# Moving columns of the last rows from VectorE to GpSimd, and recutting the last row

## The chip, the cores and the metric

One core of a Trainium2 chip. The metric is the device time of one execution in microseconds. One execution of each kernel is also profiled; it gives the trace, whose span is 1.77 us shorter than the time of the same execution (628.57 against 626.8 for the kernel before). A load's *landing* is the moment of its last completion event in the trace.

## The reference

```python
def setup_inputs():
    return {"x": np.random.randn(8192, 8192).astype(np.float32)}

def reference(x):
    return np.linalg.norm(x, ord=np.inf, axis=1)
```

That is the largest absolute value of each row of 268 MB of float32. Every byte is read once and 32 KB are written.

## The kernel before

The kernel handles 128 rows of x at a time, one per partition (a "row" below is such a group of 8192 columns per partition; a "pair" is two of them in one transfer). SyncE issues all loads into a ring of three pairs, and VectorE takes the absolute maximum along the columns. For the last pair and the last two rows GpSimd helps: ScalarE makes the values positive in place, then GpSimd takes the maximum of their bits as integers. The constants give, per transfer, its columns and GpSimd's share of them:

```python
TILES = (
    [[(8192, 0)]] * HEAD
    + [[(16384, 0)]] * (PAIRS - 1)
    + [[(16384, 7168)], [(8192, 3328)]]
    + [[(4160, 1760), (2080, 832), (1024, 384), (512, 0), (416, 0)]]
)
```

VectorE gets the rest of each transfer. The last row comes in five pieces. Each share of it leaves one partial maximum behind the last piece's columns in the tile `last`, and one final reduce takes the piece and the partial maxima together:

```python
            if final:                                   # the last piece of the last row
                pairs_out()
                absmax(res[:, R - 1 :], last)           # its columns and the partial maxima
            elif u == len(TILES) - 1:                   # the other pieces of the last row
                for eng, a, e in ((absmax, 0, w - g), (absmax_pool, w - g, w)):
                    if a < e:
                        i = w_last + n_part
                        red = eng(last[:, i : i + 1], buf[:, a:e])
                        n_part += 1
                        # (cut: the matmuls of warm())
            # (cut: whole rows for VectorE alone)
            else:                                       # the last pair, and the row before the last
                part = single.tile([P, 2], FP32, name=f"part{u}")
                c = w // n_cols - 1
                if c:
                    absmax(res[:, row : row + c], buf[:, : c * n_cols])
                red = absmax(part[:, 0:1], buf[:, c * n_cols : w - g])
                absmax_pool(part[:, 1:2], buf[:, w - g :])
                max_pool(res[:, row + c : row + c + 1], part)
```

After the final reduce TensorE transposes the last four rows' results, ScalarE copies them out of PSUM and a small store ends the kernel.

## Time and profile before

| kernel before | |
|---|---|
| time, median of 3 (lowest, highest) | 628.57 us (628.52, 628.62) |
| span of the profiled execution | 626.8 us |
| start of VectorE's 8192 reduce of the last pair | 603.28 us |
| end of the final reduce | 624.14 us |
| between the two, called the **tail** below | 20.86 us |
| end of the final reduce to end of span | 2.66 us |

The first 603 us are a stream of loads, which the change doesn't touch. What the change can move is the tail. It is worked out from lines rounded to 0.01 us. The time of an execution is the sum 603.28 + 20.86 + 2.66 + 1.77 = 628.57. The profile's lines are read in the prediction.

### The profile page before, as it was taken

Reading aid. Unit: us, or ns where it says so; the run is one execution under the profiler, and the core shown is the slowest. Engines: PE = TensorE matmul, PEld = TensorE weight load, DVE = VectorE, ACT = ScalarE, POOL = GpSimd, SP = SyncE. Lnnn points to the kernel's source line nnn. Section 1 sums busy time; section 2 is a strip of 40 time slices with the busy share of each in tenths; the row PEclk is TensorE's granted clock in tenths of the full one; section 3 lists DMA queues with packets and bytes.
Section 4 is the critical chain, followed back from the end, with each engine's and each line's share of the span. In section 5 each row is a group of like instructions: output and inputs, shape, how many; then the busy total and the mean of one; then the engine's idle time right before and its main releaser. Section 6 shows DMA issues by size and latency. Waiting matters only on the chain.

```text
span 626.8 us, 218 instructions
## 1 busy us (share of the span) xinstructions
PE 8.7 (1%) x15; PEld 3.2 (1%) x15; DVE 537.5 (86%) x39; ACT 14.3 (2%) x10; POOL 13.3 (2%) x13
## 2 busy tenths in 40 slices
PE   0000000000000000000000000000000000000005
PEld 0000000000000000000000000000000000000002
DVE  1938988889988889888898888988889988889888
ACT  0000000000000000000000000000000000000034
POOL 0000000000000000000000000000000000000007
PEclk9999999999999999999999999999999999999999
DMA  8999999999999999999999999999999999999996
GB/s 368 435 468 402 468 402 468 402 468 402 468 402 468 402 460 410 452 418 448 422 448 422 418 452 402 468 402 468 402 468 402 468 402 468 402 468 402 460 402 278
DMA packets 5525, 268.47 MB, mean 428 GB/s; under 512 B 627, under 2 KB 789, under 8 KB 1045
## 3 DMA queue, kind: packets, MB, share of 16 engines
q1 hardware_dynamic: 5472, 268.44, 99.1%
q10 hardware_dynamic: 53, 0.03, 0.0%
HBM read 268.44 MB, written 0.03 MB: 428 GB/s over the span
## 4 chain that ended last, share of the span: by engine, by line
DMA 70%; DVE 29%; issue 0%; SPq 0%; PE 0%; ACT 0%; DVEq 0%
DMA ring<-in_x_dram 70%; DVE res L64 28%; DVE part L64 1%; DVE last L64 1%; SPq L153 0%; PE ps_ones L189 0%; ACT sb_ones L190 0%; DVEq L64 0%
## 5 line engine op out<-in xcount | busy, mean ns | idle before, releaser
L64 DVE TENSOR_REDUCE res<-ring 128x2 f32<-128x16384 f32 (+1 forms) x32 | 525.4, 16420 | 86.5 <-DMA ring<-in_x_dram 86.5
L82 ACT ACTIVATE ring<-ring 128x7168 f32<-128x7168 f32 (+4 forms) x5 | 12.2, 2449 | 577.0 <-DMA ring<-in_x_dram 577.0
L71 POOL TENSOR_REDUCE part<-ring 128x1 int32<-128x7168 int32 (+1 forms) x2 | 9.1, 4566 | 587.3 <-ACT ring L82 587.2
L108 PE MATMUL ps_warm<-ident 128*128 128x512 f32 (+1 forms) x12 | 8.2, 827 | 614.5 <-DVE part L64 613.2
L64 DVE TENSOR_REDUCE part<-ring 128x1 f32<-128x1024 f32 (+1 forms) x2 | 6.3, 3210 | 0.0
L108 PEld LDWEIGHTS ps_warm<-ident 128*128 128x128 f32 x12 | 2.9, 274 | 618.8 <-issue 615.3
L64 DVE TENSOR_REDUCE last<-ring 128x1 f32<-128x2400 f32 (+3 forms) x4 | 5.3, 1392 | 0.0
L71 POOL TENSOR_REDUCE last<-ring 128x1 int32<-128x1760 int32 (+2 forms) x3 | 3.0, 1017 | 0.4 <-ACT ring L82 0.4
L96 ACT ACT_TABLE_LOAD x1 | 1.3, 1283 | 31.5 <-DVE res L64 31.5
L64 DVE TENSOR_REDUCE res<-last 128x1 f32<-128x423 f32 x1 | 0.6, 594 | 0.1
L88 POOL MEMSET ident<- 128x128 f32 x1 | 0.2, 205 | 21.4 <-DVE res L64 21.4
L128 ACT COPY sb_pairs<-ps_pairs 30x128 f32<-30x128 f32 x2 | 0.4, 254 | 0.0
L71 POOL TENSOR_REDUCE res<-part 128x1 int32<-128x2 int32 x2 | 0.4, 196 | 0.1
L123 PE MATMUL ps_pairs<-ident,res 128*30 128x128 f32 x2 | 0.4, 272 | 0.0
L190 ACT COPY sb_ones<-ps_ones 4x128 f32<-4x128 f32 x1 | 0.3, 255 | 2.0 <-PE ps_ones L189 2.0
masks.py:199 POOL TENSOR_SCALAR_AFFINE_SELECT ident<-ident 128x128 f32<-128x128 f32 x1 | 0.3, 294 | 0.1
L189 PE MATMUL ps_ones<-ident,res 128*4 128x128 f32 x1 | 0.3, 272 | 1.3 <-DVE res L64 1.3
L123 PEld LDWEIGHTS ps_pairs<-ident,res 128*30 128x30 f32 x2 | 0.2, 106 | 0.6 <-POOL res L71 0.3
L96 ACT ACTIVATE ident<-ident 128x1 f32<-128x1 f32 x1 | 0.2, 203 | 0.0
L208 POOL MEMSET const-float32-0.0<- 128x1 f32 x1 | 0.1, 99 | 0.2 <-issue 0.2
L208 POOL MEMSET const-bfloat16-1.0<- 128x1 bf16 x1 | 0.1, 102 | 0.0
L208 POOL MEMSET const-uint8-127<- 128x1 uint8 x1 | 0.1, 102 | 0.0
(2 smaller groups left out, 0.2 us busy)
## 6 DMA issues: line engine op xcount, KB each, us to landing
ring<-in_x_dram SPq DMA_DIRECT2D x3, 4096.0 KB, 21.5
ring<-in_x_dram SPq DMA_DIRECT2D x1, 2080.0 KB, 35.7
ring<-in_x_dram SPq DMA_DIRECT2D x1, 1040.0 KB, 37.8
ring<-in_x_dram SPq DMA_DIRECT2D x1, 512.0 KB, 38.5
ring<-in_x_dram SPq DMA_DIRECT2D x30, 40.8
ring<-in_x_dram SPq DMA_DIRECT2D x1, 256.0 KB, 38.7
last<-in_x_dram SPq DMA_DIRECT2D x1, 208.0 KB, 38.7
out_dram<-sb_pairs ACTq DMA_DIRECT2D x1, 30.0 KB, 1.5
```

Of the source, the lines that this page charges most:

```text
L64: return keep(nc.vector.tensor_reduce(out=dst, in_=src, axis=X, op=MAX, apply_absolute_value=True,)).ins
L71: keep(pool.add_instruction(mybir.InstTensorReduce(name=nc.get_next_instruction_name(), ins=[pool.lower_ap(src.bitcast(INT32))], outs=[poo ...
L82: keep(nc.scalar.activation(src, src, mybir.ActivationFunctionType.Abs))
L88: nc.gpsimd.memset(ident, 0.0).ins, after.name,
L96: abs_ident = nc.scalar.activation(ident[:, :1], ident[:, :1], mybir.ActivationFunctionType.Abs)
L108: product = keep(nc.tensor.matmul(ps_warm[:, : w * P], lhsT=ident, rhs=ident.unsqueeze(1).to_broadcast([P, w, P]), start=True, stop=True,) ...
L123: keep(nc.tensor.transpose(ps_pairs[r], both[:, :, r], ident))
L128: keep(nc.scalar.copy(sb[:, :, r], ps_pairs[r]))
L189: nc.tensor.transpose(ps_ones, res[:, X_ONE:], ident)
L190: keep(nc.scalar.copy(sb_ones, ps_ones))
L208: nc = _bacc.Bacc("TRN2", target_bir_lowering=False, num_devices=1)
```

## The change

Its intent is to relieve VectorE at the end of the kernel: GpSimd's shares grow by 2 to 8 per cent, and the last row is recut so that its last piece is larger and its first two smaller.

```diff
-    + [[(16384, 7168)], [(8192, 3328)]]
-    + [[(4160, 1760), (2080, 832), (1024, 384), (512, 0), (416, 0)]]
+    + [[(16384, 7328)], [(8192, 3488)]]
+    + [[(4128, 1824), (2048, 864), (1024, 416), (512, 0), (480, 0)]]
```

## The prediction

> **What bounds the kernel now.** I read four views in this order: the page's span and chain that ended last, the chain in order of time for the tail, the timeline of the last 24 us, and the groups by form for durations. The page says who holds the end in bulk:
>
> ```profile
> span 626.8 us, 218 instructions
> ...
> DMA 70%; DVE 29%; issue 0%; SPq 0%; PE 0%; ACT 0%; DVEq 0%
> ...
> q1 hardware_dynamic: 5472, 268.44, 99.1%
> ```
>
> The input queue keeps the 16 DMA engines busy 99.1% of the span. The 29% of VectorE (DVE) in the chain doesn't mean that VectorE bounds the stream: a load waits there for a ring buffer to be released, and other loads are in flight meanwhile. The change touches no load before the last row, so only the tail matters:
>
> ```profile
> 562.46 40.80 DMA ring<-in_x_dram
> ...
> 603.28 8.69 DVE res L64
> 611.97 6.25 DVE part L64 x2
> 618.22 5.25 DVE last L64 x4
> ...
> 623.55 0.60 DVE res L64
> ...
> 624.20 0.28 PE ps_ones L189
> ...
> 624.51 0.26 ACT sb_ones L190
> ```
>
> Columns: start, length, what. From 603.28 to 624.16 VectorE works with no gap. It is the engine that sets the end of the tail, and after it come only a transpose, a copy and the store. The timeline shows how close the others are:
>
> ```profile
> 603.28 8.69 DVE L64 TENSOR_REDUCE res<-ring 128x1 f32<-128x8192 f32 x1 [2.14 <-DMA ring<-in_x_dram]
> 603.36 6.18 ACT L82 ACTIVATE ring<-ring 128x7168 f32<-128x7168 f32 x1 [570.36 <-DMA ring<-in_x_dram]
> ...
> 613.04 2.98 ACT L82 ACTIVATE ring<-ring 128x3328 f32<-128x3328 f32 x1 [3.50 <-DMA ring<-in_x_dram]
> ...
> 617.97 1.67 ACT L82 ACTIVATE ring<-ring 128x1760 f32<-128x1760 f32 x1 [1.95 <-DMA ring<-in_x_dram]
> ...
> 619.71 3.08 POOL L71 TENSOR_REDUCE last<-ring 128x1 int32<-128x1760 int32 x3 [0.38 <-ACT ring L82]
> 620.45 0.90 ACT L82 ACTIVATE ring<-ring 128x832 f32<-128x832 f32 x1 [0.81 <-DMA ring<-in_x_dram]
> ...
> 621.68 0.52 ACT L82 ACTIVATE ring<-ring 128x384 f32<-128x384 f32 x1 [0.34 <-DMA ring<-in_x_dram]
> ```
>
> ScalarE (ACT) starts 0.02 to 0.07 us after a piece lands, so these lines give the landings. The landing events of the trace put them at 603.26 (last pair), 612.97 (8192 columns), 617.94 (4160), 620.43 (2080), 621.66 (1024), 622.29 (512) and 622.80 (416). GpSimd (POOL) ends its last reduce at 619.71 + 3.08 = 622.79. VectorE finishes its last partial reduce at 623.46 and starts the final one at 623.55. So before the final reduce the last landing has 0.75 us to spare and GpSimd 0.76 us: VectorE alone is late, and shifting columns to GpSimd is aimed at the right engine.
>
> The durations of one instruction (last number):
>
> ```profile
> L64 DVE TENSOR_REDUCE part<-ring 128x1 f32<-128x4864 f32 x1 | 5.2, 5209 | 0.0
> ...
> L64 DVE TENSOR_REDUCE last<-ring 128x1 f32<-128x512 f32 x1 | 0.7, 675 | 0.0
> ...
> L64 DVE TENSOR_REDUCE res<-last 128x1 f32<-128x423 f32 x1 | 0.6, 594 | 0.1
> ...
> L71 POOL TENSOR_REDUCE part<-ring 128x1 int32<-128x7168 int32 x1 | 6.2, 6164 | 587.2 <-ACT ring L82 587.2
> ...
> L71 POOL TENSOR_REDUCE last<-ring 128x1 int32<-128x384 int32 x1 | 0.5, 509 | 0.0
> ```
>
> VectorE: (5209 - 675) / (4864 - 512) = 1.042 ns a column plus 142 ns (the final one 153). GpSimd: (6164 - 509) / (7168 - 384) = 0.834 ns plus 189. ScalarE's 6176 ns for 7168 and 524 for 384 give 0.833 ns plus 204.
>
> **What the Trainium skill says.** "SBUF — State Buffer", section "Who interferes with whom": VectorE and GpSimd share a port pair, but a tensor_reduce on trn2 never takes it. The trace agrees: the 4864 reduce beside a busy GpSimd follows the same line (1.042 ns a column) as the 8192 reduce of an early row that ran without it (8686 ns, mean of three). So longer GpSimd shares should not slow VectorE. "Perfetto Trace Analysis", section "Optimizing Scalar/DVE Operations": about 60 ns of engine time for a VectorE instruction on SBUF, the profiled latency about twice that, the write-acknowledgement half overlapping the next. The trace agrees: the constant is 142 ns, and the next reduce starts 80 ns before the former ends (613.01 + 5.21 = 618.22 against a start at 618.14), which leaves 62. "TensorE: Matmul & The Clock Gate", Part 1: the array falls to half clock after an idle window of about 3.4 us. The warming matmuls end near 622.9 and the last transpose comes at 624.20, so the gap of 1.3 us is safe. "HBM Reference", Specifications: a core streaming alone measures about 425 GB/s; the page shows a mean of 428.
>
> **The change, part by part.** No instruction and no byte is added or removed. VectorE's own shares become 16384 - 8192 - 7328 = 864 (was 1024), 8192 - 3488 = 4704 (was 4864), 4128 - 1824 = 2304 (was 2400), 2048 - 864 = 1184 (was 1248), 1024 - 416 = 608 (was 640), 512 as before, and the final 480 + 7 partial maxima = 487 (was 423). That is 512 columns off VectorE and 64 back. At 1.042 ns, 448 columns would be 0.47 us if nothing else stood in the way. The landings do, once. I replay the tail, starting each reduce at the later of "0.08 before the former ends" and "0.02 after the landing" (603.28 against 603.26). Landings in the row of pieces move earlier by the columns no longer ahead of them, at (622.80 - 612.97) / 8192 = 1.20 ns a column: 0.04 us for the first piece, 0.08 for the next three, nothing for the last.
>
> - 864: starts 611.88 as before, lasts 0.90 + 0.14 = 1.04, ends 612.92; VectorE is free at 612.84, but the 8192 piece lands at 612.97. Of the 0.167 us won, only 0.02 is kept.
> - 4704: 612.99 + 5.04 = 618.03. Free at 617.95; landing 617.90. Won 0.167.
> - 2304: 617.95 + 2.54 = 620.49. Free at 620.41; landing 620.35. Won 0.100.
> - 1184: 620.41 + 1.375 = 621.785. Free at 621.705; landing 621.58. Won 0.067.
> - 608: 621.705 + 0.775 = 622.48. Free at 622.40; landing 622.21. Won 0.033.
> - 512: 622.40 + 0.675 = 623.075; the final starts 0.09 later, at 623.165; its piece is in at 622.80.
> - Final, 487: 0.507 + 0.153 = 0.66, ends 623.825. Lost 0.067.
>
> Sum: -0.02 - 0.167 - 0.100 - 0.067 - 0.033 + 0.067 = -0.32 us against the old end of 624.14. The transpose, copy and store follow unchanged. 628.57 - 0.32 = 628.25 us.
>
> GpSimd has to be checked on the same clock. ScalarE's 7328 ends at 603.36 + 6.31 = 609.67, GpSimd starts 0.07 later and takes 6.30, to 616.04; its small merge and the 3488 (3.10 us) follow by about 619.46; the second merge; the 1824 at about 619.78 (it now waits for GpSimd itself, no longer for ScalarE's 1824, done near 619.66). The three last shares are 128 columns longer, 0.107 us, so it ends near 619.78 + 3.08 + 0.11 = 622.97, 0.18 later than before and 0.2 before the final reduce can start. The slack is spent, not exceeded.
>
> **The rivals.** First, landings as the new bound. For it: after the change VectorE reaches the 4128 piece only 0.05 us after it lands, and the 8192 piece before it lands. Against it: a landing 0.1 us late would cost only the missing 0.05, because each later piece leaves more room. It would make about 628.3. Second, GpSimd as the last to finish. For it: its margin falls from 0.76 to about 0.2 us, and spans on it are rough. Against it: its durations lie on one line over 7168 to 384 columns. If it ran 0.4 us later than I have it, the final reduce would start 0.2 later: 628.45, still under the old time. Third, the larger final piece: the final reduce is the one step that can't lie beside anything, and 64 columns more cost 0.067 there; that is in the sum. Had VectorE been waiting for the last landing, this would be the whole effect, 628.64; the 0.75 us of slack speaks against it. Fourth, a change of the DMA stream by the new piece widths. Its 16-engine share is already 99.1%, and pieces of 4160, 2080 and 1024 columns landed at one pace (1.19 to 1.21 ns a column), so I expect nothing.
>
> **Range and chances.** The effect is 0.05%. The three runs before lie within 0.1 us, but 620 us of stream ahead of the tail may shift by some tenths in another run or on another chip, which is more than the effect. Hence 628.25, with 627.8 to 628.75 for 8 in 10. A 2% change is 12.6 us; nothing in the last 24 us can give it, and no earlier load is altered, so within 2% gets 0.99.
>
> **What would show it.** The profile after should have: an idle time of VectorE of about 0.1 us before the 4704 reduce, released by the DMA, and no other in the tail; the 487 reduce at about 660 ns; the gap from the start of the reduce at 603.28 to the end of the final one shorter by 0.3 us (20.86 to 20.54); GpSimd's last reduce ending 0.1 to 0.3 us before the final reduce starts. I am wrong if the final reduce waits for GpSimd or for a DMA, if the last transpose leaves its 272 ns, or if the landings from 603.26 to 622.80 (19.54 us) stretch by over 0.2 us.

## The result, and the profile after

| | before | after |
|---|---|---|
| time, median (lowest to highest), 6 runs each | 628.58 us (628.52 to 628.62) | 628.28 us (628.17 to 628.48) |
| start of the 8192 reduce | 603.28 | 603.39 |
| tail | 20.86 | 20.55 |
| end of final reduce to end of span | 2.66 | 2.66 |

The ratio is 0.9996 with a 95% interval of 0.9983 to 1.0009. (A ratio is the mean time of one kernel's runs over that of the other's of the same rounds, so not quite the ratio of the medians.) The medians differ by 0.30 us and the tails by 0.31. All six runs after lie below all six before (628.48 against 628.52), but the interval includes 1.

The chain of waits for the tail of the kernel after (start, length, what):

```profile
581.93 31.14 DMA ring<-in_x_dram
613.08 0.02 issue
613.10 5.05 DVE part L64
618.15 5.05 DVE last L64 x4
...
623.28 0.67 DVE res L64
```

Before, the chain ran on VectorE from 603.28 on. Now its VectorE part begins at 613.10, right after the landing of a load: the 8192 columns of the row before the last. VectorE was ready for them and waited. From there to 623.94 it has no gap but the 0.1 us before the final reduce, which was there before.

The timeline of the kernel after (start, length, engine, line, operation, shapes; in brackets idle time and what ended it):

```profile
603.39 8.69 DVE L64 TENSOR_REDUCE res<-ring 128x1 f32<-128x8192 f32 x1 [2.13 <-DMA ring<-in_x_dram]
...
618.00 1.72 ACT L82 ACTIVATE ring<-ring 128x1824 f32<-128x1824 f32 x1 [1.74 <-DMA ring<-in_x_dram]
...
619.79 3.04 POOL L71 TENSOR_REDUCE last<-ring 128x1 int32<-128x1824 int32 x3
```

GpSimd's last three shares end at 619.79 + 3.04 = 622.83, which is 0.45 us before the final reduce starts at 623.28. Its share of the 4128 piece starts 0.07 us after ScalarE has finished it (618.00 + 1.72 = 619.72).

The groups by form (the last two numbers before the second bar are busy us and mean ns, the last one idle us before it):

```profile
L71 POOL TENSOR_REDUCE part<-ring 128x1 int32<-128x7328 int32 x1 | 6.3, 6295 | 587.4 <-ACT ring L82 587.4
...
L64 DVE TENSOR_REDUCE part<-ring 128x1 f32<-128x4704 f32 x1 | 5.1, 5052 | 0.1
...
L64 DVE TENSOR_REDUCE last<-ring 128x1 f32<-128x2304 f32 x1 | 2.5, 2543 | 0.0
...
L64 DVE TENSOR_REDUCE res<-last 128x1 f32<-128x487 f32 x1 | 0.7, 660 | 0.1
```

The durations are within 0.01 us of the ones worked out beforehand: 5.05, 2.54 and 0.66 us for 4704, 2304 and 487 columns. The 0.1 us of idle time before the 4704 reduce is the wait for the landing.

### The profile page after: what moved, and what is told of

It is laid out like the page before. It is cut to its first block, busy times and chain, and to the rows that moved or that the text cites. A ratio compares the mean times of both kernels' runs of the same rounds, so it can differ in the third digit from the quotient of the medians.

```text
span 626.6 us, 218 instructions
## 1 busy us (share of the span) xinstructions
PE 8.5 (1%) x15; PEld 3.1 (0%) x15; DVE 537.1 (86%) x39; ACT 14.7 (2%) x10; POOL 13.5 (2%) x13
## 4 chain that ended last, share of the span: by engine, by line
DMA 70%; DVE 29%; SPq 0%; issue 0%; PE 0%; ACT 0%; DVEq 0%
DMA ring<-in_x_dram 70%; DVE res L64 28%; DVE part L64 1%; DVE last L64 1%; SPq L153 0%; PE ps_ones L189 0%; ACT sb_ones L190 0%; DVEq L64 0%
## 5 line engine op out<-in xcount | busy, mean ns | idle before, releaser
L82 ACT ACTIVATE ring<-ring 128x7328 f32<-128x7328 f32 (+4 forms) x5 | 12.6, 2524 | 576.5 <-DMA ring<-in_x_dram 576.5
L71 POOL TENSOR_REDUCE part<-ring 128x1 int32<-128x7328 int32 (+1 forms) x2 | 9.4, 4697 | 587.4 <-ACT ring L82 587.4
L64 DVE TENSOR_REDUCE part<-ring 128x1 f32<-128x864 f32 (+1 forms) x2 | 6.1, 3047 | 0.1
L64 DVE TENSOR_REDUCE last<-ring 128x1 f32<-128x2304 f32 (+3 forms) x4 | 5.1, 1342 | 0.0
L71 POOL TENSOR_REDUCE last<-ring 128x1 int32<-128x1824 int32 (+2 forms) x3 | 3.0, 1052 | 0.1
```

What stands on the lines that cost most here:

```text
L64: return keep(nc.vector.tensor_reduce(out=dst, in_=src, axis=X, op=MAX, apply_absolute_value=True,)).ins
L71: keep(pool.add_instruction(mybir.InstTensorReduce(name=nc.get_next_instruction_name(), ins=[pool.lower_ap(src.bitcast(INT32))], outs=[poo ...
L82: keep(nc.scalar.activation(src, src, mybir.ActivationFunctionType.Abs))
```

## The experiments

**Theory.** VectorE's chain of reduces sets the end. A column taken off it is worth 1.04 ns, unless VectorE then reaches a piece before it has landed; a column added to the final reduce costs as much. GpSimd has slack. **Rivals:** the new piece widths, not the shares, are what helped; every column off VectorE counts in full, landings or not; GpSimd is already at its limit, or its late start holds the end.

Each run below gives the tail of its profiled execution and the median of its timed ones. Unless it says otherwise, an edit is to the kernel after. The kernel before had a median of 628.66 us (628.54 to 629.19; nine runs in the first call, and these with one more in the second) and of 628.54 (628.38 to 629.17; the same nine runs serve the third and the fourth). Each tail is of one execution, and how far the tail of one kernel scatters was not measured. Four kernels from which the theory expects nearly the same tail (the kernel after, and the runs first_share_back, first_share_larger and shares_in_halves below) came out at 20.55 to 20.56 us.

### The two halves of the change by themselves

The shares without the new pieces:

```diff
-    + [[(4128, 1824), (2048, 864), (1024, 416), (512, 0), (480, 0)]]
+    + [[(4160, 1856), (2080, 896), (1024, 416), (512, 0), (416, 0)]]
```

> The larger GpSimd shares with the old pieces (4160, 2080, 1024, 512, 416): VectorE's partial reduces are those of the changed kernel (864, 4704, 2304, 1184, 608, 512) and its final one is 423 again. Tail = start of VectorE's 8192 reduce in the last pair to the end of the final reduce (20.86 us before, 20.55 after). My theory (VectorE's chain, cut short by landings): 0.07 us is saved on the final reduce, but the old pieces land 0.04 to 0.08 later, so VectorE waits some 0.03 us before the 2304 and again before the 1184 reduce; tail 20.53 to 20.57, 628.25 to 628.30 us, as good as the whole change. Rival 1 (the piece widths are what helped): tail near 20.86, 628.58. Rival 2 (VectorE's columns alone count, no landings): 20.55 - 0.07 = 20.48, 628.21.

Measured: tail 20.53 us; 628.27 us (628.22 to 628.30), ratio 0.9993 (0.9980 to 1.0007). The 2304 and 1184 reduces became 9 and 10 ns longer (2552 and 1386), which the theory does not name; they also start where VectorE meets the landing. From its timeline:

```profile
603.31 8.69 DVE L64 TENSOR_REDUCE res<-ring 128x1 f32<-128x8192 f32 x1 [2.12 <-DMA ring<-in_x_dram]
...
623.25 0.59 DVE L64 TENSOR_REDUCE res<-last 128x1 f32<-128x423 f32 x1
```

The pieces without the shares:

```diff
-    + [[(16384, 7328)], [(8192, 3488)]]
-    + [[(4128, 1824), (2048, 864), (1024, 416), (512, 0), (480, 0)]]
+    + [[(16384, 7168)], [(8192, 3328)]]
+    + [[(4128, 1760), (2048, 832), (1024, 384), (512, 0), (480, 0)]]
```

> The new piece widths with GpSimd's old shares: VectorE's partial reduces 1024, 4864, 2368, 1216, 640, 512 and a final 487, in sum as many columns as before (32 + 32 less, 64 more). My theory: tail 20.86 us, 628.58 us, no gain. Rival 1 (the piece widths are what helped, by the stream or by the landings): tail near 20.55, 628.28.

Measured: tail 20.86 us; 628.49 us (628.38 to 628.66), ratio 0.9997 (0.9985 to 1.0010). From its timeline:

```profile
603.10 8.69 DVE L64 TENSOR_REDUCE res<-ring 128x1 f32<-128x8192 f32 x1 [2.13 <-DMA ring<-in_x_dram]
...
623.30 0.66 DVE L64 TENSOR_REDUCE res<-last 128x1 f32<-128x487 f32 x1
```

In this profile, of an execution of 628.38 us, the 8192 reduce starts at 603.10, 0.18 us earlier than in the kernel before, so the 0.17 us between the medians lies in the stream ahead of the tail as far as the profiled execution can tell. What follows from the two: the shares give the whole gain. The new cut gives none. It does one thing that is hidden: the last landing comes 19.49 us after the pair's in this run and after, against 19.53 and 19.54 with the old widths, but nobody waits for it.

### Is each column off VectorE worth its time?

The last pair's share put back:

```diff
-    + [[(16384, 7328)], [(8192, 3488)]]
+    + [[(16384, 7168)], [(8192, 3488)]]
```

> The changed kernel with GpSimd's share of the last pair back at 7168, so that VectorE's 864 reduce is 1024 again. My theory: the wait of about 0.1 us for the 8192 piece before the 4704 reduce goes, and only 0.01 to 0.03 us is lost: tail 20.56 to 20.58 us, 628.28 to 628.31. Rival (every column taken off VectorE is worth its 1.04 ns): 160 columns, 0.17 us longer, tail 20.72, 628.45.

Measured: tail 20.56 us; 628.29 us (628.19 to 628.69), ratio 0.9995 (0.9983 to 1.0008). The groups by form of this run show no idle time before the 4704 reduce:

```profile
L64 DVE TENSOR_REDUCE part<-ring 128x1 f32<-128x4704 f32 x1 | 5.0, 5044 | 0.0
```

So 160 columns more on VectorE cost 0.01 us, not 0.17. And the other way, 320 columns fewer:

```diff
-    + [[(16384, 7328)], [(8192, 3488)]]
+    + [[(16384, 7648)], [(8192, 3488)]]
```

> The changed kernel with 320 more columns for GpSimd in the last pair (7648), so that VectorE's 864 reduce becomes 544. My theory: VectorE then waits some 0.45 us instead of 0.12 for the 8192 piece and the tail (start of VectorE's 8192 reduce in the last pair to the end of the final reduce) stays 20.55 us; GpSimd ends 0.26 us later and still ahead of the final reduce; 628.28 us. Rival (each column off VectorE is worth 1.04 ns): tail 20.22, 627.95. Rival (GpSimd is already at its limit): tail 20.8.

Measured: tail 20.55 us; 628.2 us (628.06 to 628.67), ratio 0.9993 (0.9981 to 1.0006). The timeline of VectorE in this run:

```profile
611.73 0.71 DVE L64 TENSOR_REDUCE part<-ring 128x1 f32<-128x544 f32 x1
612.84 5.05 DVE L64 TENSOR_REDUCE part<-ring 128x1 f32<-128x4704 f32 x1 [0.40 <-DMA ring<-in_x_dram]
```

The 0.33 us that the shorter reduce saves turn into idle time, and the profile names the load that ends it. A miss in the detail: GpSimd ended 19.86 us after the start of the 8192 reduce, 0.42 later than in the kernel after and not 0.26, so that it and VectorE were ready for the final reduce together. The expectation had counted the 320 columns on GpSimd alone; ScalarE's step on the share, which comes first, took 0.27 us longer too (6.58 us against 6.31), and a later wait for ScalarE that fell away took back some 0.13. Both runs tell the same: the gain of the kernel after is cut short at the landing of the 8192 piece, and what the last pair's share does beyond that is worth nothing.

### How near is GpSimd to its limit?

```diff
-    + [[(4128, 1824), (2048, 864), (1024, 416), (512, 0), (480, 0)]]
+    + [[(4128, 1984), (2048, 1024), (1024, 576), (512, 0), (480, 0)]]
```

> The changed kernel with 160 more columns for GpSimd in each of the 4128, 2048 and 1024 pieces (1984, 1024, 576). My theory: GpSimd takes the place of VectorE as the last before the final reduce. Its last reduce ends 0.40 us later (480 columns at 0.834 ns) and the final reduce waits for it, with VectorE also waiting 0.1 to 0.15 us at landings; tail 20.65 to 20.83 us, so slower than the changed kernel by 0.1 to 0.28: 628.38 to 628.56. Rival (VectorE's columns count alone): 480 columns, 0.50 us shorter, tail 20.05, 627.8. Rival (landings alone bound it): tail near 20.4, as VectorE then is ready 0.16 us earlier.

Measured: tail 20.69 us; 628.6 us (628.18 to 628.92), ratio 0.9998 (0.9986 to 1.0011). From the timeline of this run:

```profile
620.33 3.44 POOL L71 TENSOR_REDUCE last<-ring 128x1 int32<-128x1984 int32 x3 [0.22 <-ACT ring L82]
...
623.80 0.66 DVE L64 TENSOR_REDUCE res<-last 128x1 f32<-128x487 f32 x1 [0.41 <-POOL last L71]
```

VectorE's final reduce sits idle 0.41 us until GpSimd's last share is there (620.33 + 3.44 = 623.77). This is the first bracket of that kind on the final reduce. Beyond some size of the shares, then, more columns for GpSimd lengthen the tail, and 480 columns more are beyond it. A miss in the detail: GpSimd ended 0.55 us later than in the kernel after (20.00 us after the start of the 8192 reduce) and not 0.40; the bracket of 0.22 us shows that it waited for ScalarE, whose step on the larger share is longer as well.

```diff
-    + [[(16384, 7328)], [(8192, 3488)]]
-    + [[(4128, 1824), (2048, 864), (1024, 416), (512, 0), (480, 0)]]
+    + [[(16384, (3664, 3664))], [(8192, (1744, 1744))]]
+    + [[(4128, (896, 928)), (2048, (864,)), (1024, (416,)), (512, ()), (480, ())]]
```

(and a loop over the parts of a share, each with its own Abs, its own maximum and its own column among the partial maxima)

> The changed kernel with GpSimd's shares of the last pair, of the 8192 piece and of the 4128 piece each cut in two (3664 + 3664, 1744 + 1744, 896 + 928), so that GpSimd starts 3 us earlier, after ScalarE's first half. My theory (VectorE sets the end, GpSimd has slack): GpSimd gets idle time, ends about as before, VectorE's times don't change; tail 20.53 to 20.57, 628.28 us. Rival (GpSimd's late start is what holds the end): tail at least 0.1 us shorter, below 20.45.

Measured: tail 20.56 us; 628.23 us (628.17 to 628.44), ratio 0.9993 (0.9980 to 1.0007). GpSimd in this run:

```profile
606.59 6.43 POOL L71 TENSOR_REDUCE part<-ring 128x1 int32<-128x3664 int32 x2 [584.37 <-ACT ring L82]
...
614.66 3.23 POOL L71 TENSOR_REDUCE part<-ring 128x1 int32<-128x1744 int32 x2 [1.38 <-ACT ring L82]
...
618.81 1.84 POOL L71 TENSOR_REDUCE last<-ring 128x1 int32<-128x896 int32 x2 [0.53 <-ACT ring L82]
```

Counted from the start of the 8192 reduce (603.18 here, 603.39 there), it starts 3.05 us earlier than in the kernel after (3.41 us after it, not 6.46), and it gets idle time of 1.38 and 0.53 us instead, waiting for ScalarE, which waits for landings. The tail stays. GpSimd's late start doesn't hold the end.

### Versions meant to beat both

If VectorE reaches the final piece 0.4 us after it has landed, more columns may go from VectorE's earlier pieces to GpSimd and into the final piece. Constants only:

```diff
-    + [[(16384, 7328)], [(8192, 3488)]]
-    + [[(4128, 1824), (2048, 864), (1024, 416), (512, 0), (480, 0)]]
+    + [[(16384, 7328)], [(8192, 3552)]]
+    + [[(4064, 1824), (1984, 896), (1024, 480), (512, 0), (608, 0)]]
```

> Only the constants of the last rows: GpSimd 7328 and 3552; pieces 4064, 1984, 1024, 512, 608 with GpSimd 1824, 896, 480. My theory says that in the changed kernel the final piece lies in SBUF some 0.4 us before VectorE gets to it; so more columns can move from VectorE's earlier pieces to GpSimd and into the final piece until its reduce starts as it lands (VectorE 864, 4640, 2240, 1088, 544, 512, final 615). Expected: final reduce starts 0.3 us earlier than in the changed kernel and takes 0.79 us; tail 20.38 us (20.35 to 20.45), 628.08 to 628.15 us. Rival (the final piece must stay small, as its reduce lies beside nothing): tail 20.65 or more.

Measured: tail 20.39 us, the shortest of all; but 628.37 us (628.16 to 628.49), ratio 0.9995 (0.9981 to 1.0009). From its timeline:

```profile
603.56 8.69 DVE L64 TENSOR_REDUCE res<-ring 128x1 f32<-128x8192 f32 x1 [2.14 <-DMA ring<-in_x_dram]
...
623.16 0.79 DVE L64 TENSOR_REDUCE res<-last 128x1 f32<-128x615 f32 x1
```

The expectation for the tail holds and that for the time doesn't. In the profiled execution the stream was late: 603.56 + 20.39 + 2.65 + 1.77 = 628.37. The start of the 8192 reduce ranged from 603.10 to 603.77 over all profiled executions, more than any difference of tails here. So the median of five runs can't rank these versions.

Then the parts in halves, with a sixth piece to make the last reduces smaller:

```diff
-    + [[(16384, 7328)], [(8192, 3488)]]
-    + [[(4128, 1824), (2048, 864), (1024, 416), (512, 0), (480, 0)]]
+    + [[(16384, (5664, 1664))], [(8192, (1840, 1968))]]
+    + [[(4128, (832, 1088)), (1952, (512, 480)), (896, (544,)), (352, ()), (352, ()), (512, ())]]
```

> A version meant to beat both: GpSimd's large shares in two parts (5664 + 1664, 1840 + 1968, 832 + 1088, 512 + 480), and the last row in six pieces of 4128, 1952, 896, 352, 352 and 512 columns, so that VectorE reaches the final piece as it lands. VectorE 864, 4384, 2208, 960, 352, 352, 352 and a final 522. My theory: the final reduce starts within 0.05 us of the last landing and takes 0.70 us; tail 20.24 us (20.2 to 20.35), 627.95 to 628.05 us. Rivals: a sixth piece slows the last landings by over 0.1 us, or one of the shorter GpSimd parts comes late: tail 20.4 or more.

Measured: tail 20.44 us; 628.17 us (627.97 to 628.53), ratio 0.9993 (0.9979 to 1.0006). From its timeline:

```profile
623.16 0.70 DVE L64 TENSOR_REDUCE res<-last 128x1 f32<-128x522 f32 x1 [0.20 <-DMA last<-in_x_dram]
```

A miss: the final reduce waits for the last landing. That came at 623.03, 19.64 us after the pair's where the runs with five pieces had until then 19.47 to 19.54, and the reduce started 0.13 us after it, not 0.02. About 0.10 us of the 0.20 by which the tail missed its 20.24 are this wait (the idle time is 0.20 us, in the kernel after 0.10). The rest came earlier: the three reduces of 352 columns each started 0.02 to 0.03 us after their pieces had landed, and these landed late too. The first rival, a slower stream with a sixth piece, had come true in its number. Two runs went after its cause:

```diff
-    + [[(4128, 1824), (2048, 864), (1024, 416), (512, 0), (480, 0)]]
+    + [[(4128, 1824), (2048, 864), (1024, 416), (256, 0), (256, 0), (480, 0)]]
```

> The changed kernel with the 512 piece cut into 256 + 256, which adds one transfer and one VectorE reduce and leaves all else: a look at what a sixth piece costs by itself. In every run with five pieces the last landing came 19.47 to 19.54 us after the landing of the last pair; in the six-piece run 19.64. Theory A (a sixth transfer costs time in the stream): last landing 19.57 to 19.65 us after the pair's. Theory B (the widths of 352, 1952 and 896 columns in that run, or that run alone): 19.47 to 19.51. Either way VectorE sets the end, 0.06 us later than in the changed kernel for one more reduce: tail 20.60 to 20.63 us.

Measured (one look): tail 20.62 us, 628.29 us, last landing 19.51. A sixth transfer by itself cost the stream nothing to speak of here (19.51 against 19.49); the tail is longer by the one more reduce.

```diff
-    + [[(16384, 7328)], [(8192, 3488)]]
-    + [[(4128, 1824), (2048, 864), (1024, 416), (512, 0), (480, 0)]]
+    + [[(16384, (5664, 1664))], [(8192, (1808, 1808))]]
+    + [[(4096, (736, 1120)), (2048, (576, 448)), (896, (576,)), (384, ()), (384, ()), (384, ())]]
```

> The six-piece version again with widths in whole multiples of 128 columns (4096, 2048, 896, 384, 384, 384), a smaller final piece, and its shares set for a final reduce that starts 0.1 us after the last landing (GpSimd 5664 + 1664, 1808 + 1808, 736 + 1120, 576 + 448, 576). VectorE reaches the final reduce 19.71 us after the start of its 8192 reduce; it lasts 0.56. If the last landing is at 19.5 to 19.6 after the pair's: tail 20.27 to 20.32 us, about 628.0 to 628.1 us, the best of all. If the three small pieces land 0.1 us late or more, as in the first six-piece version, VectorE waits for each of them: tail 20.38 or more, no better than the version with retuned constants (20.39).

Measured: tail 20.49 us; 628.12 us (628.09 to 628.52), ratio 0.9993 (0.9979 to 1.0007). The last landing is at 19.74 us, later still, and VectorE started both of its 384 reduces 0.02 us after their pieces had landed, as the expectation had it for late landings. By its median this is the fastest kernel of the study, 0.42 us under the kernel before of the same call, but its interval too includes 1, and its tail is longer than that of the retuned constants. Even widths were no cure. The last two split the suspicion in two:

```diff
-    + [[(4128, 1824), (2048, 864), (1024, 416), (512, 0), (480, 0)]]
+    + [[(4096, 1792), (2048, 864), (1024, 416), (512, 0), (512, 0)]]
```

> A look at where the late last landing of the two six-piece versions comes from (19.64 and 19.74 us after the pair's, 19.47 to 19.54 in all the others). The changed kernel with pieces of 4096, 2048, 1024, 512 and 512 columns (GpSimd 1792, 864, 416): the 2048 piece now starts at column 4096, as in the even six-piece version, where it landed 2.53 us after the piece before it and not 2.43. If that start is the cause: 2.5 us again and a last landing at 19.55 or later. If not: 2.43 and 19.47 to 19.52. VectorE sets the end either way: tail 20.57 to 20.60 us.

Measured: tail 20.60 us, 628.4 us.

```diff
-    + [[(4128, 1824), (2048, 864), (1024, 416), (512, 0), (480, 0)]]
+    + [[(4128, 1824), (2048, 864), (864, 480), (384, 0), (384, 0), (384, 0)]]
```

> The same question from the other side: pieces of 4128, 2048, 864, 384, 384 and 384 columns (GpSimd 1824, 864, 480), with the shares whole. If three small pieces in a row are the cause, each lands more than 0.48 us after the one before (384 columns at 1.20 ns are 0.46) and the last at 19.6 or later; if not, at 19.47 to 19.52. VectorE sets the end either way (partials 384, 384, 384, final 392): tail 20.53 to 20.60 us, no gain over the changed kernel.

Measured: tail 20.56 us, 628.34 us. The landings of the pieces after that of the last pair, from the landing events of the traces (us; one profiled execution each):

| run | pieces | landings |
|---|---|---|
| after | 4128, 2048, 1024, 512, 480 | 14.61, 17.04, 18.26, 18.89, 19.49 |
| one piece split | 4128, 2048, 1024, 256, 256, 480 | 14.61, 17.03, 18.27, 18.59, 18.92, 19.51 |
| powers of two | 4096, 2048, 1024, 512, 512 | 14.62, 17.12, 18.42, 19.10, 19.69 |
| three small last | 4128, 2048, 864, 384, 384, 384 | 14.62, 17.06, 18.15, 18.67, 19.18, 19.64 |
| six pieces, even | 4096, 2048, 896, 384, 384, 384 | 14.60, 17.13, 18.25, 18.76, 19.28, 19.74 |

Each suspect alone made the last landing late: with a 4096 piece in front, the next 2048 columns take 2.50 us and not 2.43, the 1024 after them 1.30 and not 1.22, and the end comes 0.20 us later; with three pieces of 384 columns the first two take 0.52 and 0.51 us, where 1.20 ns a column make 0.46. The even version, which has both, is the latest. With the 4096 piece the packets of one size are themselves slower: in the DMA records of the traces those of 2048 bytes took 87 ns in the mean against 84 in the kernel after, those of 8192 bytes 313 against 309. Why they are slower is open: each rests on one look, and no run took a mechanism away.

## Why the prediction was right

**What sets the end.** "VectorE alone is late" before the change: shown. The shares alone shorten the tail by 0.33 us, and the new cut alone leaves it at 20.86.

**The wait at the 8192 piece.** Of the first 160 columns only 0.02 us was to be kept. Shown from both sides: giving them back costs 0.01, and taking 320 more gives 0.00, the profile naming the load.

**The sum.** Predicted -0.32 us, a tail of 20.54 and 628.25 us; measured -0.31, 20.55 and 628.28. The reduces have the durations worked out, the final one 660 ns as foretold. The other four VectorE savings weren't taken apart by runs; their sum, with the one wait, agrees.

**GpSimd.** Its margin before the final reduce shrank, as foretold, but to 0.45 us and not to 0.2, which is outside the 0.1 to 0.3 given as a sign; and its end, foretold 0.18 us later, came 0.06 us sooner (19.445 us after the start of the 8192 reduce, 19.505 before). The mis-sized terms are waits for ScalarE that the replay carried over from the trace before. There GpSimd's shares of 3328, 832 and 384 columns each started 0.07 us after ScalarE had finished them; in the kernel after GpSimd came to them later and found them ready. So the 3488 share started 0.11 us earlier than worked out, and in "619.78 + 3.08 + 0.11" the three last shares took 3.04 us and not 3.19. The words "it now waits for GpSimd itself, no longer for ScalarE's 1824" fell too: the start at 619.79 is still 0.07 us after ScalarE's end, and in the run with 7648 columns, where ScalarE had long been done with that share, GpSimd started it 0.06 us before its merge ended. That the error fell on the safe side is luck: 0.24 us the other way would have made GpSimd the last by some 0.05 us. So the rival "GpSimd as the last" was farther off than stated, and it comes true with 480 columns more.

**The DMA stream.** "I expect nothing" from the piece widths was nearly so: the last landing came 0.06 us earlier (19.486 us after the pair's, 19.543 before), hidden, and the four before it 0.07 to 0.14 us earlier, where 0.04 to 0.08 had been worked out. As a rule it would have been wrong: other widths moved the last landing by 0.2.

**Readings.** Three are loose, and none enters the sum. ScalarE's "0.02 to 0.07 us after a piece lands" doesn't hold for the pair (603.26 to 603.36). "No gap" from 603.28 on leaves out the 0.09 us before the final reduce, which the replay does count. And of the three 8192 reduces only two are of early rows; beside the third GpSimd ran for its last 2.4 us, but each of the three took 8686 ns. The last transpose kept its 272 ns.

**The range.** 627.8 to 628.75 held every one of the six runs. What filled it was the stream, as said: the tail's change of 0.31 us is no larger than the scatter of one kernel's own executions.

## What to carry to other kernels

When a row of reduces on one engine ends the kernel, replay it with two numbers per instruction (time per column and fixed part) and the landing of each piece; a column moved off the engine pays only up to the next landing. Judge such changes by a stretch of the trace that leaves out the part that scatters: here the medians of a few runs didn't rank versions whose tails differed by 0.1 to 0.2 us in 628. After recutting pieces, look at where the last one lands: widths at powers of two and three last pieces of 384 columns each made it later, while cutting one piece of 512 columns in two did not.

## What the Trainium skill lacked or had wrong

- "DMA: Bandwidth & Descriptors", section "Latency and other measured facts", has copies between tensors in HBM that are slower at row pitches of large powers of two: 207 GB/s at 512 KiB down to 103 at 4 MiB. Here the pieces of the last row have a pitch of 32 KiB, and the cut of the row alone moved the last landing: 19.49 us after the pair's with 4128, 2048, 1024, 512, 480 columns, 19.69 with 4096, 2048, 1024, 512, 512 (one look each). No page has it.
- "GPSIMD Engine Reference", section 4.1, sends every reduce along the free dimension to VectorE. Here GpSimd's integer maximum over 128 partitions took 0.834 ns a column plus 189 ns, less per column than VectorE's absolute maximum (1.042 ns plus 142), though it needs ScalarE to take the absolute value first.
- "Perfetto Trace Analysis", section "Identifying Dependency Chains", says that an instruction which waits on several engines may have further semaphore instructions ahead of it, and gives no cost. Here VectorE started 0.02 us after a landing when it waited for that alone, and 0.13 us after it in the first six-piece version, where the final reduce depends on VectorE's and GpSimd's partial maxima too.
